# Scores of a two-head attention tile: the products of queries' high parts with keys' low parts move to 64 rows of TensorE each

## Chip, cores and metric

The kernel runs on one core of a Trainium2 chip. The metric is the device time of one launch in microseconds (us). The kernel before takes 1949.45 us, the median of three runs that lie between 1949.08 and 1949.52.

## What is computed

Two layers on 1024 tokens of width 1024, in float32: a gated short convolution and a SwiGLU feed-forward, then banded attention and a second feed-forward. The change lies in the attention. Each of 16 query heads has 64 channels; four query heads share one of four key heads; a block of 128 queries sees its own block of keys and the one before.

```python
    q = rmsnorm(q, q_gain)
    k = rmsnorm(k, k_gain)
    ...
    scores = jnp.einsum('bnqkgd,bnskd->bnkgqs', qb, kw).astype(jnp.float32) * scale
    ...
    logits = jnp.concatenate([scores, sink_col], axis=-1)
    p = jax.nn.softmax(logits, axis=-1)[..., :-1]
    out = jnp.einsum('bnkgqs,bnskd->bnqkgd', p.astype(vw.dtype), vw)
    out = out.reshape(bsz, s, N_Q_HEADS * HEAD_DIM)
    return out @ w_o
```

## The kernel before

**Split products.** TensorE multiplies in the type fp32r, which keeps less than float32. So each float32 matrix is split into a high part (rounded to fp32r) and a low part (the rest), and a product is the sum of high x high, high x low and low x high. `product_step` does this for one 128-row slice of the sum: six 128x512 matmuls, high weights on the two halves of the tokens with the operand's high part, again with its low part (L165), and the low weights with the high part (L169). `product` is a generator that hands back control after every two matmuls. The two halves of the tokens (512 columns each) go to two banks of PSUM that carry the tag `acc`; there are four of these, taken in turn, so that one product is summed while the other's two banks are read. Four other banks are called P0 to P3.

**A query tile.** The queries are projected in eight tiles i of 128 channels, each of which holds two heads e = 0 and 1 (64 channels each). `keep_q` copies the projected tile out of its two `acc` banks (`squares`, L1653, and `copy`, L1643, both on ScalarE), scales it by the heads' norms, and makes one operand for each head: 128 rows, of which the head's own 64 (rows 0 to 63 for e = 0, 64 to 127 for e = 1) hold the high part of its queries, and the other 64 the low part of the same queries. The keys stand twice, on rows 0 to 63 and on rows 64 to 127, as high part `hi` and low part `lo`.

**Scores.** `scores(i, b)` makes the scores of both heads of tile i for query block b, into the two halves of bank P0. For each head it issues two matmuls of 128 rows by 256 keys: the operand with `hi` (L1724), which gives high x high and low x high at once, and the operand with `lo` (L1725), which gives high x low and, as a by-product, low x low. There are 8 x 8 = 64 such units (i, b), so 256 matmuls. VectorE reads the scores in `maxima` (L1746, one instruction for each head, with the distance bias, the mask and the running minimum). Then ScalarE makes the exponents (L1764), TensorE transposes them (`turn`, L1776) into P1 or P3, ScalarE and VectorE split them (L1783, L1789), TensorE multiplies them with the values (L1801, L1802) into P2, and `keep_o` adds the two results (L1818, L1819).

**Order.** The attention's main part is ordered by hand: the program order of TensorE, VectorE, ScalarE and GpSimd is the order in which the code issues. `step` is called eight times for each query tile. It issues the scores of unit n, the transposes of unit n - 2 and the value products of unit n - 3 (LAG sets how the units run behind the projections), and between these three pieces of the running projection (P in the string below, two matmuls each). `plan(d, f)` puts f into an agenda d steps ahead; a whole number is issued at the end of that step (K), one with .5 in its middle (k).

```python
ORDER = "SPTZMEDkPHLBVOPK"
```

The letters are: S scores, T transposes, Z the preparation of the next score buffer, M maxima, E exponents, D divisions, H and L the split of the exponents, B the blanking of a column, V value products, O their sum.

For query tiles 1 to 7 the projection of tile i runs beside the attention of the tiles before. When it is done, the first half of the output projection follows: eight tiles m of output channels, each a product over the four operands in `o_split`, four steps for each m, with `add_x` (L282, VectorE) adding the two banks to the residual. `split_o` (L1912 on ScalarE, L1913 on GpSimd) makes those operands, in the room of the projections' operands XS0 to XS2 while query tile 7 is still being projected. Other tiles' head norms use `head_stats` (L1513, matmuls of two columns) and `turn_blocks` (L1601, transposes).

Of the kernel before, what the change touches and what calls it, by code (L numbers as in the profile page):

```python
# [10 lines left out]
F32 = mybir.dt.float32  # L11
# [70 lines left out]
def trunk_kernel(ctx: ExitStack, tc: tile.TileContext, xT, small, w_in, w_out, w_qk, w_v, w_o, w_gu, w_dn, out):  # L82
# [2 lines left out]
    pm = ctx.enter_context(tc.tile_pool(name="pm", bufs=1, space=bass.MemoryType.PSUM))  # L85
    dve, act, pool, pe = nc.vector, nc.scalar, nc.gpsimd, nc.tensor
    uid = [0]

    def slot(tag, shape=(P, D), dtype=F32, bufs=1):
        uid[0] += 1  # L90
# [4 lines left out]

    def bank(tag):
        uid[0] += 1
        return pm.tile([P, 512], F32, tag=tag, name=f"{tag}_{uid[0]}", bufs=4 if tag == "acc" else 1)

    def plain(ap):  # L100
        return ap.bitcast(F32)
# [40 lines left out]
    def load_w(src, n, hi_eng=act, lo_eng=dve):  # L142
        w = Weights()
        w.load(src, 0, n)
        w.split(0, n, hi_eng, lo_eng)
        return w
# [3 lines left out]
    class Acc:  # L150


        def __init__(self, tags=("acc", "acc")):
            self.parts = [(bank(tags[h]), slice(h * 512, h * 512 + 512)) for h in (0, 1)]

        def half(self, h):
            return self.parts[h][0]
# [1 line left out]
    def product_step(ps, w, xs, k, first, last):  # L159
        wh = w.hi[:, k * P : (k + 1) * P]  # L160
        wl = w.lo[:, k * P : (k + 1) * P]
        for j in (0, 1):
            for h in (0, 1):
                c = slice(h * 512, h * 512 + 512)
                pe.matmul(ps.half(h), wh, xs[:, j, c], start=first and j == 0, stop=False)  # L165
            yield
        for h in (0, 1):
            c = slice(h * 512, h * 512 + 512)
            pe.matmul(ps.half(h), wl, xs[:, 0, c], start=False, stop=last)  # L169
        yield  # L170

    def product(ps, w, operands, n=None):
        n = n or len(operands)
        for k in range(n):
            yield from product_step(ps, w, operands[k], k, k == 0, k == n - 1)

    def run(gen):
        for _ in gen:
# [1319 lines left out]
    def attention_layer():  # L1498
# [136 lines left out]
        def keep_q(i, acc):  # L1635

            t = {}

            def copy(h):
                if h == 0:  # L1640
                    t["raw"] = slot("G7") if i + 1 < NK else t["both"][:, 0, :]
                src, c = acc.parts[h]
                act.copy(t["raw"][:, c], src)  # L1643

            def squares(h):
                if h == 0:
                    if i + 1 < NK:
                        side = slot(f"G{5 + i % 2}")
                    else:
                        t["both"] = slot("XS5", (P, 2, D))  # L1650
                        side = t["both"][:, 1, :]
                    t["side"] = [side[:, h * 512 : h * 512 + 512] for h in (0, 1)]
                act.activation(t["side"][h], acc.half(h), AF.Square)  # L1653

            def stats_of():
                t["st"] = bank(pos["free"])
                for h in (0, 1):
                    head_stats(t["st"], t["side"][h], 4 * h, 4)

            def mean():  # L1660
                t["m"] = head_mean(t["st"])
                t["y"] = head_log(t["m"])

            def guess():
                t["t"] = head_guess(t["y"], cst[:, C_INVS + 2 * i : C_INVS + 2 * i + 2])

            def newton():
                head_newton(t["y"], t["t"], t["m"])


            def halves(e):
                rows = [slice(0, HD), slice(HD, P)]
                return rows[e], rows[1 - e]

            def part_hi(h, e):
                rows, _ = halves(e)
                if h == 0 and e == 0:
                    Q[i] = [slot(f"G{3 + i % 2}", dtype=F32R), slot(f"G{5 + i % 2}", dtype=F32R)]
                c = slice(h * 512, h * 512 + 512)
                dve.tensor_copy(Q[i][e][rows, c], t["raw"][rows, c])  # L1680

            def part_lo(h, e):
                rows, rest = halves(e)
                c = slice(h * 512, h * 512 + 512)
                q = Q[i][e]
                pool.tensor_tensor(q[rest, c], t["raw"][rows, c], plain(q)[rows, c], ALU.subtract)

            rows_of = lambda h: scale_rows(t["raw"], t["side"][h], h, bank(pos["free"]))
            wide_of = lambda h: spread(act, t["side"][h], t["y"][:, 4 * h : 4 * h + 4, :])

            first, rows = (1, (4.5, 5.5)) if i + 1 < NK else (0, (5.5, 6.5))
            for d, fs in (
                (first, [lambda: squares(0)]),
                (first + 0.5, [lambda: squares(1)]),
                (1.5 + first, [stats_of, mean]),
                (2 + first, [guess, newton]),
                (rows[0] - 1.5 if first else 0, [lambda: copy(0)]),
                (rows[0] - 1, [lambda: wide_of(0)]),
                (rows[0] - 0.5 if first else 1, [lambda: copy(1)]),
                (rows[0], [lambda: wide_of(1)]),  # L1700
                (rows[0], [lambda: rows_of(0)]),
                (rows[1], [lambda: rows_of(1)]),
                (rows[1], [lambda: part_hi(0, 0), lambda: part_hi(0, 1)]),
                (rows[1] + 0.5, [lambda: part_lo(0, 0)]),
                (rows[1] + 1, [lambda: part_lo(0, 1)]),
                (rows[1] + 1.5, [lambda: part_hi(1, 0), lambda: part_hi(1, 1), lambda: part_lo(1, 0)]),
                (rows[1] + 2.5, [lambda: part_lo(1, 1)]),
            ):
                for f in fs:
                    plan(d, f)  # L1710

        def key_blocks(b):
            return [1] if b == 0 else [0, 1]

        def scores(i, b):
            hi, lo = kz[i // 4]
            g = i % 2
            k0 = max(b - 1, 0)
            n = (b + 1 - k0) * P
            t = slice(b * P, (b + 1) * P)  # L1720
            kc = slice(k0 * P, (k0 + 2) * P)
            ps = bank("P0").rearrange("p (e c) -> p e c", e=2)
            for e, q in enumerate(Q[i]):
                pe.matmul(ps[:, e, :], q[:, t], hi[:, g, kc], start=True, stop=False)  # L1724
                pe.matmul(ps[:, e, :], q[:, t], lo[:, g, kc], start=False, stop=True)  # L1725
            S[i, b] = {"ps": ps, "n": n}


# [9 lines left out]
        def maxima(i, b):  # L1738
            u = S[i, b]
            s = u["s"] = s_bufs[(i * NB + b) % 3]  # L1740
            lo = 2 * P - u["n"]
            skip = 1 if lo == 0 else 0
            mx = u["mx"] = slot("mx", (P, 2), bufs=3)
            for e in range(2):
                h = 2 * i + e
                dve.tensor_tensor_reduce(  # L1746
                    s[:, e, lo + skip :],
                    u["ps"][:, e, skip : u["n"]],
                    dist[:, lo + skip :],
                    cst[:, C_NEGS + h : C_NEGS + h + 1],  # L1750
                    sinks[:, h : h + 1],
                    ALU.add,
                    ALU.min,
                    mx[:, e : e + 1],
                )
# [197 lines left out]
        E = mybir.EngineType  # L1953
        with tc.manual_schedule(engines={E.PE, E.Activation, E.DVE, E.Pool}):
            keep_q(0, acc)
            w = load_w(w_qk[1], NK, dve, pool)

            def load_next(i):
# [6 lines left out]

            w_after = load_next(2)
            for i in range(1, NK):
                acc = Acc()
                work = product(acc, w, xs)
                for k in range(NK):  # L1970
                    if k == 0:
                        w_next, w_after = w_after, None
                        n_next = NK if i + 1 < NK else len(early)
                    if k == 4 and i + 1 < NK:
                        w_after = load_next(i + 2)
                    if i == 6 and k == 2:
                        split_o(0, "A0", 0)
                    if i == 7 and k in (1, 3, 5):
                        split_o((k + 1) // 2, f"XS{k // 2}", 0)
                    step(work)  # L1980
                    if k in (0, 2, 3, 5):
                        j = 2 * (0, 2, 3, 5).index(k)
                        if j < n_next:
                            w_next.split(j, 2, act, pool)
                run(work)
                keep_q(i, acc)
                w = w_next
# [2 lines left out]
            free = ["XS3", "XS4"]  # L1990
            first_w = {}
            for m in range(NK):
                acc = Acc()
                work = product(acc, w, o_split, len(early))
                for k in range(len(early)):
                    if m + 1 < NK and k == 0:
                        w_next = Weights()
# [21 lines left out]
            while agenda:  # L2019
                planned_early()  # L2020
                planned()

        begin_with = []
        for e in (0, 1):
# [116 lines left out]
```

## Time and profile before

| | |
|---|---|
| median of three runs | 1949.45 us (1949.08 to 1949.52) |
| the profiled execution | 1950.02 us, span 1948.3 us |
| TensorE matmuls, busy share of the span | 99% |
| TensorE weight loads (beside the matmuls) | 83% |
| VectorE | 71% |
| ScalarE | 44% |
| GpSimd | 13% |
| attention's scores (L1724) | first at 1042.7 us, last at 1251.0 us |

PE is TensorE's matmul side and PEld its weight-load side; DVE is VectorE, ACT ScalarE, POOL GpSimd. A matmul's recorded time runs from its start to the end of its result, so neighbouring matmuls overlap in the record: what a stream of them costs is the distance from one start to the next. A time before a source line's group is busy time, then the mean of one instruction in ns, then the idle time ahead of it and what ended it.

### The profile page before, as it was taken

Reading aid. Unit: us, or ns where it says so; the run is one execution under the profiler, and the core shown is the slowest. Engines: PE = TensorE matmul, PEld = TensorE weight load, DVE = VectorE, ACT = ScalarE, POOL = GpSimd, SP = SyncE. Lnnn points to the kernel's source line nnn. Section 1 sums busy time; section 2 is a strip of 40 time slices with the busy share of each in tenths; the row PEclk is TensorE's granted clock in tenths of the full one; section 3 lists DMA queues with packets and bytes.
Section 4 is the critical chain, followed back from the end, with each engine's and each line's share of the span. In section 5 each row is a group of like instructions: output and inputs, shape, how many; then the busy total and the mean of one; then the engine's idle time right before and its main releaser. Section 6 shows DMA issues by size and latency. Waiting matters only on the chain.

```text
span 1948.3 us, 25757 instructions
## 1 busy us (share of the span) xinstructions
PE 1938.1 (99%) x9153; PEld 1617.3 (83%) x9153; DVE 1389.9 (71%) x2520; ACT 861.4 (44%) x1678; POOL 249.7 (13%) x384
## 2 busy tenths in 40 slices
PE   9999999999999999999999999999999999999999
PEld 7888888888888888888898888888888888888887
DVE  8998767876767676675645887788676767675543
ACT  5543434533333335444435777656333333344432
POOL 0000011011111110000004454410111111110000
PEclk9999999999999999999999999999999999999999
DMA  8532185244565458976300000051454555388563
GB/s 312 169 98 87 65 301 185 86 161 173 175 205 185 162 177 284 329 258 208 100 22 23 23 12 18 28 194 60 168 194 170 176 205 178 126 284 278 191 229 102
DMA packets 143169, 311.81 MB, mean 160 GB/s; under 512 B 13888, under 2 KB 53952, under 8 KB 143040
## 3 DMA queue, kind: packets, MB, share of 16 engines
q1 hardware_dynamic: 118992, 225.71, 35.0%
q0 software_dynamic: 23904, 84.42, 11.8%
q8 instruction: 72, 1.18, 0.3%
q14 instruction: 57, 0.47, 0.1%
q10 hardware_dynamic: 144, 0.03, 0.0%
HBM read 219.40 MB, written 90.70 MB: 159 GB/s over the span
## 4 chain that ended last, share of the span: by engine, by line
PE 93%; DVE 4%; issue 1%; ACT 1%; DMA 1%; SPq 0%; DVEq 0%; ACTq 0%
PE acc L907 15%; PE acc L904 15%; PE acc L905 15%; PE P L904 9%; PE P L907 9%; PE P L905 9%; PE acc L165 6%; PE acc L169 3%; PE acc L1034 2%; PE acc L1032 2%; PE acc L1033 2%; PE P L1776 1%; PE P L1724 1%; PE P L1513 1%; PE P L1601 1%
## 5 line engine op out<-in xcount | busy, mean ns | idle before, releaser
L904 PE MATMUL acc<-XS,G 128*128 128x512 f32 x894 | 348.2, 389 | 0.0
L907 PE MATMUL acc<-XS,G 128*128 128x512 f32 x894 | 347.8, 389 | 0.0
L905 PE MATMUL acc<-XS,G 128*128 128x512 f32 x894 | 347.8, 389 | 0.0
L905 PEld LDWEIGHTS acc<-XS,G 128*128 128x128 f32 x894 | 167.8, 188 | 34.8
L907 PEld LDWEIGHTS acc<-XS,G 128*128 128x128 f32 x894 | 167.8, 188 | 34.8
L904 PEld LDWEIGHTS acc<-XS,G 128*128 128x128 f32 x894 | 167.8, 188 | 34.8
L905 PE MATMUL P<-A,G 128*128 128x512 f32 x502 | 195.3, 389 | 0.0
L904 PE MATMUL P<-A,G 128*128 128x512 f32 x502 | 195.3, 389 | 0.0
L907 PE MATMUL P<-A,G 128*128 128x512 f32 x502 | 195.3, 389 | 0.0
L904 PE MATMUL acc<-A,G 128*128 128x512 f32 x410 | 159.5, 389 | 0.0
L905 PE MATMUL acc<-A,G 128*128 128x512 f32 x410 | 159.5, 389 | 0.0
L907 PE MATMUL acc<-A,G 128*128 128x512 f32 x410 | 159.5, 389 | 0.0
L844 DVE TENSOR_TENSOR G<-WL,G 128x512 fp32r<-128x512 f32 x168 | 115.0, 685 | 53.0 <-ACT G L843 53.0
L165 PE MATMUL acc<-XS,WH 128*128 128x512 f32 x480 | 146.8, 405 | 0.9 <-ACT WH L137 0.8
L843 ACT CAST G<-WR 128x512 fp32r<-128x512 f32 (+1 forms) x198 | 119.7, 605 | 62.9 <-PE acc L907 27.7
L844 DVE TENSOR_TENSOR G<-WR,G 128x512 fp32r<-128x512 f32 (+1 forms) x198 | 131.9, 666 | 10.9 <-ACT G L843 10.5
L843 ACT CAST G<-WH 128x512 fp32r<-128x512 f32 (+1 forms) x156 | 93.7, 601 | 82.9 <-PE acc L907 38.1
L1204 ACT ACTIVATE G<-G 128x512 f32<-128x512 f32 x88 | 55.8, 634 | 162.0 <-DVE G L1275 157.9
L843 ACT CAST G<-WL 128x512 fp32r<-128x512 f32 x168 | 103.5, 616 | 37.4 <-DVE WL L787 33.6
L904 PE MATMUL P<-XS,G 128*128 128x512 f32 x290 | 112.9, 389 | 0.1
L907 PE MATMUL P<-XS,G 128*128 128x512 f32 x290 | 112.8, 389 | 0.0
L905 PE MATMUL P<-XS,G 128*128 128x512 f32 x290 | 112.8, 389 | 0.0
(318 smaller groups left out, 3914.6 us busy)
## 6 DMA issues: line engine op xcount, KB each, us to landing
G<-h SPq DMA_DIRECT2D x70, 512.0 KB, 5.3
h<-X POOLq DMA_DIRECT2D x44, 512.0 KB, 5.2
X<-in_w_dn SPq DMA_DIRECT2D x80, 256.0 KB, 3.5
s<-X POOLq DMA_DIRECT2D x40, 512.0 KB, 4.7
WR<-in_w_gu SPq DMA_DIRECT2D x36, 512.0 KB, 6.1
WH<-in_w_gu SPq DMA_DIRECT2D x36, 512.0 KB, 6.4
h<-X POOLq DMA_DIRECT2D x66, 256.0 KB, 4.1
WR<-s SPq DMA_DIRECT2D x52, 256.0 KB, 3.4
```

The costliest lines, as they stand in the source:

```text
L165: pe.matmul(ps.half(h), wh, xs[:, j, c], start=first and j == 0, stop=False)
L169: pe.matmul(ps.half(h), wl, xs[:, 0, c], start=False, stop=last)
L843: lambda: act.copy(out_hi, raw),
L844: lambda: lo_eng.tensor_tensor(out_lo, raw, plain(out_hi), ALU.subtract),
L904: pe.matmul(ps, w[:, 0, c], x[:, 0, :], start=start and e == 0, stop=False, skip_group_check=True)
L905: pe.matmul(ps, w[:, 0, c], x[:, 1, :], start=False, stop=False, skip_group_check=True)
L907: pe.matmul(ps, w[:, 1, c], x[:, 0, :], start=False, stop=last, skip_group_check=True)
L1032: pe.matmul(ps, hi[:, kc], xs[:, 0, c], start=k == 0, stop=False, skip_group_check=True)
L1033: pe.matmul(ps, hi[:, kc], xs[:, 1, c], start=False, stop=False, skip_group_check=True)
L1034: pe.matmul(ps, lo[:, kc], xs[:, 0, c], start=False, stop=k == n_op - 1, skip_group_check=True)
L1204: state["silu"] = act.activation(x, x, AF.Silu)
L1513: pe.matmul(st[:, o : o + 2], sq[:, b * P : (b + 1) * P], half, start=True, stop=True)
```

## The change

In `scores` the two high matmuls of 128 rows come first, head 0 into bank P0 and head 1 into another bank. Then the two matmuls with `lo` follow, each on 64 rows only: head 0's high query rows (0 to 63) with the copy of the keys' low part on rows 0 to 63, at row position 0 of TensorE, and head 1's on rows 64 to 127, at row position 64. They add to what the high matmuls put into the two banks. The by-product low x low is left out. The count of matmuls stays: four for each unit.

The second bank is one of the four `acc` banks, taken out of the rotation for the length of the attention's main part and put back at its end; the rotation is written out as four tags. The projections then have three banks. So they go half by half of the tokens (`product_by_halves`): all slices of the first half into one bank, then all of the second half into the next, again with two matmuls between handings-back. The query tile 7 goes in four pieces (first half slices 0 to 3, second half slices 0 to 3, and so on). `copy(0)` of `keep_q` is planned for step 2 in place of 3 (step 1 for tile 6, step 0 for tile 7 as before), and the three `split_o` beside query tile 7 move from steps 1, 3 and 5 to 3, 4 and 5.

```diff
+    acc_tags = deque(f"acc{i}" for i in range(4))
...
     def bank(tag):
         uid[0] += 1
-        return pm.tile([P, 512], F32, tag=tag, name=f"{tag}_{uid[0]}", bufs=4 if tag == "acc" else 1)
+        if tag == "acc":
+            tag = acc_tags[0]
+            acc_tags.rotate(-1)
+        return pm.tile([P, 512], F32, tag=tag, name=f"{tag}_{uid[0]}", bufs=1)
...
+    def product_by_halves(ps, w, operands, n, chunk):
+        i = 0
+        for k0 in range(0, n, chunk):
+            for h in (0, 1):
+                c = slice(h * 512, h * 512 + 512)
+                if k0 == 0:
+                    ps.parts.append((bank("acc"), c))
+                for k in range(k0, k0 + chunk):
+                    kc = slice(k * P, (k + 1) * P)
+                    for j, (wp, xp) in enumerate(((w.hi, 0), (w.hi, 1), (w.lo, 0))):
+                        pe.matmul(
+                            ps.half(h),
+                            wp[:, kc],
+                            operands[k][:, xp, c],
+                            start=k == 0 and j == 0,
+                            stop=k == n - 1 and j == 2,
+                        )
+                        if i % 2:
+                            yield
+                        i += 1
...
-                (rows[0] - 1.5 if first else 0, [lambda: copy(0)]),
+                (0 if i + 1 == NK else 1 if i + 2 == NK else 2, [lambda: copy(0)]),
...
+        score_tags = ["P0"]
...
-            ps = bank("P0").rearrange("p (e c) -> p e c", e=2)
+            ps = [bank(tag)[:, 0 : 2 * P] for tag in score_tags]
             for e, q in enumerate(Q[i]):
-                pe.matmul(ps[:, e, :], q[:, t], hi[:, g, kc], start=True, stop=False)
-                pe.matmul(ps[:, e, :], q[:, t], lo[:, g, kc], start=False, stop=True)
+                pe.matmul(ps[e], q[:, t], hi[:, g, kc], start=True, stop=False)
+            for e, q in enumerate(Q[i]):
+                rows = slice(e * HD, (e + 1) * HD)
+                pe.matmul(ps[e], q[rows, t], lo[rows, g, kc], start=False, stop=True, tile_position=(e * HD, 0))
...
-                    u["ps"][:, e, skip : u["n"]],
+                    u["ps"][e][:, skip : u["n"]],
...
+            score_tags.append(acc_tags.popleft())
...
-                acc = Acc()
-                work = product(acc, w, xs)
+                acc = Acc(())
+                work = product_by_halves(acc, w, xs, NK, NK if i + 1 < NK else NK // 2)
...
-                    if i == 7 and k in (1, 3, 5):
-                        split_o((k + 1) // 2, f"XS{k // 2}", 0)
+                    if i == 7 and k in (3, 4, 5):
+                        split_o(k - 2, f"XS{k - 3}", 0)
...
-                acc = Acc()
-                work = product(acc, w, o_split, len(early))
+                acc = Acc(())
+                work = product_by_halves(acc, w, o_split, len(early), len(early))
...
+            acc_tags.insert(1, score_tags.pop())
```

More of the change, by code (lines that the diff above doesn't have):

```diff
@@ L153, in __init__ @@
         def __init__(self, tags=("acc", "acc")):
-            self.parts = [(bank(tags[h]), slice(h * 512, h * 512 + 512)) for h in (0, 1)]
+            self.parts = [(bank(tags[h]), slice(h * 512, h * 512 + 512)) for h in range(len(tags))]
         def half(self, h):
```

## The prediction

> **What bounds the kernel now.** The page comes first: its busy times, its row of TensorE's granted clock and the shares of the chain that ended last.
>
> ```profile
> span 1948.3 us, 25757 instructions
> PE 1938.1 (99%) x9153; PEld 1617.3 (83%) x9153; DVE 1389.9 (71%) x2520; ACT 861.4 (44%) x1678; POOL 249.7 (13%) x384
> PEclk9999999999999999999999999999999999999999
> PE 93%; DVE 4%; issue 1%; ACT 1%; DMA 1%; SPq 0%; DVEq 0%; ACTq 0%
> ```
>
> TensorE is the bound of the whole program, at its full clock, and 93% of the chain is its matmuls. The change lies in one stage, so the stage decides. Two stretches of the attention's main part, by the view of windows, and what TensorE waited for from 1042 to 1265 us, by the view of waits:
>
> ```profile
> core 0: us, PE busy (x) PEld busy (x) DVE busy (x) ACT busy (x) POOL busy (x), PEclk, DMA share, GB/s
> 1090.00:1120.00 30.00, 29.78 (x202) 26.28 (x201) 25.40 (x80) 22.95 (x70) 12.85 (x24) 1.00 0.07 19
> 1120.00:1150.00 30.00, 29.62 (x203) 26.15 (x202) 23.08 (x77) 22.54 (x70) 13.45 (x22) 1.00 0.03 10
> ```
>
> ```profile
> engine line waited for: us in total, times, longest us
> PE P L1724 <- DVE mx L1746: 1.7, 4, 0.6
> PE P L1776 <- DVE G L1768: 1.0, 3, 0.5
> PE P L1776 <- DVE s L1768: 0.3, 1, 0.3
> PE P L1776 <- ACT G L1764: 0.2, 1, 0.2
> ```
>
> TensorE is 99% busy in both stretches, and its recorded waits in 223 us come to 3.2 us. VectorE, the next engine, is at 25.40/30 = 85% and 23.08/30 = 77%. So what TensorE loses here the kernel loses, nearly one for one; what TensorE gains passes on as long as VectorE stays below its limit.
>
> **The scores now.** By source line, and then in the timeline of the two sides of TensorE:
>
> ```profile
> L1724 PE MATMUL P<-A,G x128: 274/278/356, 1042.7 to 1251.0; 128*128 128x256 f32 x128
> L1725 PE MATMUL P<-A,G x128: 274/282/283, 1042.8 to 1251.1; 128*128 128x256 f32 x128
> ```
>
> ```profile
> 1124.49 0.28 PE L1724 MATMUL P<-A,G 128*128 128x256 f32 x1
> 1124.61 0.28 PE L1725 MATMUL P<-A,G 128*128 128x256 f32 x1
> 1124.72 0.28 PE L1724 MATMUL P<-A,G 128*128 128x256 f32 x1
> 1124.85 0.28 PE L1725 MATMUL P<-A,G 128*128 128x256 f32 x1
> 1124.96 0.63 PE L165 MATMUL acc<-XS,WH 128*128 128x512 f32 x2
> ```
>
> Four matmuls of a unit take 1124.96 - 1124.49 = 0.47 us, so 0.117 us from start to start, while one lasts 0.278 us from start to end: each runs into the one before. 64 units lie between 1042.7 and 1251.0 us, one every 208.3/63 = 3.31 us.
>
> **Part 1: the pair side by side.** If the two 64-row matmuls of a unit stream at the same time, they take the place of one, and a unit loses 0.117 us: 64 x 0.117 = 7.5 us less on TensorE. No row of before has two matmuls side by side, so this gain is bounded by 0 and 7.5 us.
>
> **Part 2: going to 64 rows and back.** Each unit now changes TensorE from matmuls that use 128 rows to matmuls that use 64, and back: 128 changes. Before has no matmul on 64 rows, so the price must be bounded. From below: nothing. The nearest small price is a weight load that is not drawn ahead of the matmul it serves. It shows where the form of the work changes, from the two-column matmuls to the projection, in the timeline:
>
> ```profile
> 1122.80 0.36 PE L1513 MATMUL P<-cst,G 128*128 128x2 f32 x2
> 1123.02 0.71 PE L165 MATMUL acc<-XS,WH 128*128 128x512 f32 x2
> ```
>
> ```profile
> 1122.99 0.30 PEld L165 LDWEIGHTS acc<-XS,WH 128*128 128x128 f32 x2
> 1124.27 0.19 PEld L1724 LDWEIGHTS P<-A,G 128*128 128x128 f32 x1
> 1124.85 0.31 PEld L165 LDWEIGHTS acc<-XS,WH 128*128 128x128 f32 x2
> ```
>
> At 1124.85 the load stands 0.11 us ahead of its matmul (1124.96), and the two matmuls take 0.63 us. At 1122.99 it is 0.03 us ahead, and the same two take 0.71: 0.08 us are lost. At 0.08 for each change a unit would come to 2 x 0.08 - 0.117 = +0.043 us, and 64 units to +2.8 us.
>
> The next price is the whole tail of a matmul. If matmuls of the other form may not enter until the last has left, the distance between starts grows from 0.117 to the duration, 0.278: 0.161 us for each change. A unit then comes to 2 x 0.161 - 0.117 = +0.205 us, and 64 units to **+13.1 us**. From above: the new form's load begins only after that, too. Where TensorE starts again after a wait, the loads show what one takes:
>
> ```profile
> 1127.50 0.19 PEld L1724 LDWEIGHTS P<-A,G 128*128 128x128 f32 x1 [0.72 <-PE P L1802]
> 1127.53 0.35 PE L1724 MATMUL P<-A,G 128*128 128x256 f32 x1 [0.32 <-DVE mx L1746]
> 1127.61 0.19 PEld L1725 LDWEIGHTS P<-A,G 128*128 128x128 f32 x1
> 1127.73 0.28 PE L1725 MATMUL P<-A,G 128*128 128x256 f32 x1
> ```
>
> The second load starts 0.11 us behind the first, though nothing else held it. With 0.11 us more for each change a unit is at 2 x (0.161 + 0.11) - 0.117 = +0.425 us, and 64 units are at +27.2 us.
>
> I take the middle one. Adjacent matmuls overlap by 0.161 us, which needs both on the same 128 rows and the same way out; the two forms end differently (one sum over 128 rows against two sums over 64, in two banks), and a load of 0.11 us fits into that tail. The break-even is a price of 0.117/2 = 0.058 us for a change, below even the 0.08 of the mildest row. The Trainium skill, "TensorEngine Tiling (Array Packing)", section "Key Properties", has a rule that speaks against this change: "Changing tiling mode (not just tile) drains the TensorE". It gives no time; no run of before has two modes, so the trace neither bears it out nor denies it, and by it the middle price or the upper one would hold.
>
> **Part 3: banks and order around it.** The projections issue the same matmuls with the same loads in another order, so nothing changes in their count. They have three banks in place of four, which adds waits: the second half of tile i + 1 takes the bank of tile i's first half, behind the squares and the copy on ScalarE; in the output projection, behind the add on VectorE.
>
> ```profile
> L1653 ACT ACTIVATE G<-acc 128x512 f32<-128x512 f32 x10 | 5.9, 588 | 0.0
> L1643 ACT COPY G<-acc 128x512 f32<-128x512 f32 x12 | 6.9, 577 | 0.0
> L282 DVE TENSOR_TENSOR X<-acc,X 128x512 f32<-128x512 f32 x14 | 9.0, 687 | 0.2
> ```
>
> For tiles 2 to 6 the copy is issued at the end of the third step and wanted at the start of the fifth: one step of 3.31 us covers its 0.58. Behind a wait there TensorE would hold the transposes and value products of that step, and with them ScalarE's and VectorE's next work. Only query tile 7 has no step between: squares and copy, 0.588 + 0.577 = 1.2 us, follow the sum of the values in the step before, and the next scores (0.47 us) and value products cover half; 0 to 1.2 us, once. In the output projection the add ends 1.4 us into the second of four steps and its bank is wanted at the third. The three `split_o` now lie in adjacent steps, but end before the output projection starts, as they did. On the other side each head's scores have a bank of their own, so that head 0 need not wait for VectorE's reading of head 1: of the 1.7 us of such waits above, some may go. I put the whole part at 0, between -1.7 and +3 us. No DMA is moved, and no queue passed.
>
> **Sum.** Span 1948.3 + 13.1 = 1961.4 us; the profiled execution has 1950.02 - 1948.3 = 1.7 us around its span, so 1963.1 us. It is 0.57 us above the median 1949.45, so the median becomes **1962.5 us**, 0.7% slower. About 0.2%, 3.9 us, is what a measurement of this kernel can tell from no change.
>
> **The rivals.**
>
> *Side by side, and the change of form is free* (33%). The matmuls overlap as now, and the pair takes one's time: -7.5 us, of which VectorE at 77 to 85% lets most through; taken at 6.5, 1943.0 us. For it: TensorE already keeps a load running under the matmul before it, so work on separate rows may mix as freely; and the pair's two banks keep the outputs apart. Against it: it needs a change below 0.03 us, and the mildest visible loss is 0.08. The Trainium skill, "TensorE: Matmul & The Clock Gate", section "Part 3: Packing small matmuls", reports that matmuls on different row groups start within about 4 ns of each other; before shows none, and by that rule alone the 7.5 us would be gained.
>
> *The weight loads bind, so nothing runs side by side* (12%). A unit still has four loads. The chain of waits has a stretch of matmuls with two columns, where only the load is left:
>
> ```profile
> 1121.47 1.70 PE P L1513 x16
> ```
>
> 1.70/16 = 0.106 us for each load and matmul, close to the 0.117 of the 256-column ones. If a 64-row load takes as long and loads go one by one, the pair takes 2 x 0.106 = 0.21 us against 0.23: -1.4 us, and with a change of form at little cost 1948 to 1951 us. The change then does not do what it says. It decides where a change costs under 0.05 us.
>
> *Tail and load in line* (13%): the upper price, +27.2 us, 1976.7 us. For it: both rows above exist; against it: loads are drawn ahead almost everywhere.
>
> **How the numbers follow.** The forecast has 40%; its own range, from +3 to +22 us (a change between 0.08 and 0.23 us), is 1953 to 1972. The last 2% are waits of part 3 that exceed their cover, slower too. Faster by over 0.2% is the first rival, 0.33; within 0.2% the second, 0.12; slower the rest, 0.55. The range that should hold 8 in 10 reaches from the full gain (1949.45 - 7.5 = 1942) to just short of tail and load in line (1976): it leaves out half of that case and little else.
>
> **What would show it.** If the forecast is right, the group of 64-row matmuls starts about 0.28 us behind the high ones, its two starts lie within some 0.02 us, and the next projection starts about 0.28 us behind; the stage from first to last score grows by some 13 us, and all other stages keep their lengths. The first rival shows as 0.12, 0 and 0.12 us between starts; the second as four starts 0.11 us apart; the last as gaps near 0.39 us with loads standing behind the ends. The prediction is wrong if the scores' own spacing does not carry the difference: if TensorE waits for ScalarE or VectorE at an `acc` bank, or if a stage outside attention moves.

## The result: 1965.12 us, and the profile after

The changed kernel takes 1965.12 us (median of four runs, 1963.5 to 1966.77) against 1949.43 us of before beside it (1949.08 to 1949.52): a ratio of 1.0081, 95% interval 1.0069 to 1.0093. It is 15.7 us slower; 13.1 were forecast. The page of after, its busy times and the chain's shares:

```profile
span 1964.4 us, 25709 instructions
PE 1956.1 (100%) x9153; PEld 1621.2 (83%) x9153; DVE 1392.6 (71%) x2520; ACT 862.6 (44%) x1678; POOL 250.2 (13%) x384
PE 95%; DVE 3%; DMA 1%; ACT 1%; issue 1%; DVEq 0%; ACTq 0%
```

As many matmuls as before, and 18 us more of busy time on TensorE (1956.1 against 1938.1). The scores by source line in after, with the lowest, median and highest duration in ns and then the first and last start; L1753 is the high product, L1756 the low product on 64 rows:

```profile
L1753 PE MATMUL P<-A,G x64: 274/278/415, 1042.0 to 1266.7; 128*128 128x256 f32 x64
L1753 PE MATMUL acc<-A,G x64: 274/280/415, 1042.1 to 1266.8; 128*128 128x256 f32 x64
L1756 PE MATMUL P<-A,G x64: 379/380/579, 1042.3 to 1267.0; 64*128 64x256 f32 x64
L1756 PE MATMUL acc<-A,G x64: 379/381/577, 1042.3 to 1267.0; 64*128 64x256 f32 x64
```

From first to last score the stage now takes 1266.7 - 1042.0 = 224.7 us, where it took 208.3: that growth of 16.4 us accounts for all of the span's (1964.4 - 1948.3 = 16.1). One unit in the timeline of after, first the matmuls, then the loads:

```profile
1125.75 0.28 PE L1753 MATMUL P<-A,G 128*128 128x256 f32 x1
1125.87 0.28 PE L1753 MATMUL acc<-A,G 128*128 128x256 f32 x1
1126.08 0.38 PE L1756 MATMUL P<-A,G 64*128 64x256 f32 x1
1126.08 0.38 PE L1756 MATMUL acc<-A,G 64*128 64x256 f32 x1
1126.39 0.73 PE L192 MATMUL acc<-XS,WH 128*128 128x512 f32 x2
```

```profile
1126.08 0.18 PEld L1756 LDWEIGHTS P<-A,G 64*128 64x128 f32 x1
1126.08 0.18 PEld L1756 LDWEIGHTS acc<-A,G 64*128 64x128 f32 x1
1126.39 0.30 PEld L192 LDWEIGHTS acc<-XS,WH 128*128 128x128 f32 x2
```

The two 64-row matmuls start at the same time, so the pair does run side by side. But it starts 0.21 us behind the second high product, not 0.12; its loads begin with it and not ahead of it, and so it lasts 0.38 us and not 0.28. I read the difference, 0.10 us, as the part of the load that no matmul covers. The projection behind it stands as late again (0.31 us), with its load uncovered (0.73 us for two, where 0.63 was the rule). Leaving those 0.10 us out of the starts, a unit takes from 1125.75 to 1126.49, 0.74 us, where it took 0.47.

What TensorE still waits for in after, from 1042 to 1285 us:

```profile
PE P L1807 <- DVE G L1799: 1.1, 1, 1.1
PE acc L192 <- ACT G L1669: 0.4, 1, 0.4
```

The new waits for an `acc` bank come to 0.4 us in one place; the 3.2 us of waits of before have shrunk to 1.5.

### The profile page after: what moved, and what is told of

The parts are those of the page before. It is cut to its first block, busy times and chain, and to the rows that moved or that the text cites. A ratio compares the mean times of both kernels' runs of the same rounds, so it can differ in the third digit from the quotient of the medians.

```text
span 1964.4 us, 25709 instructions
## 1 busy us (share of the span) xinstructions
PE 1956.1 (100%) x9153; PEld 1621.2 (83%) x9153; DVE 1392.6 (71%) x2520; ACT 862.6 (44%) x1678; POOL 250.2 (13%) x384
## 4 chain that ended last, share of the span: by engine, by line
PE 95%; DVE 3%; DMA 1%; ACT 1%; issue 1%; DVEq 0%; ACTq 0%
PE acc L930 15%; PE acc L931 15%; PE acc L933 15%; PE P L930 9%; PE P L933 9%; PE P L931 9%; PE acc L192 6%; PE acc L169 2%; PE acc L1060 2%; PE acc L1058 2%; PE acc L1059 2%; PE P L1807 1%; PE acc L173 1%; PE P L1756 1%; PE P L1627 1%; PE P L1539 1%
## 5 line engine op out<-in xcount | busy, mean ns | idle before, releaser
L192 PE MATMUL acc<-XS,WH 128*128 128x512 f32 x320 | 117.7, 417 | 0.4 <-ACT G L1669 0.4
```

Source lines behind the costliest of these rows:

```text
L192: pe.matmul(ps.half(h), wp[:, kc], operands[k][:, xp, c], start=k == 0 and j == 0, stop=k == n - 1 and j == 2,)
```

## The experiments

Two theories can explain such a unit. *Change of form*: each going from 128 rows to 64 or back costs a tail and a load. *Own loads*: a 64-row matmul simply pays for its load each time. Beside them stands the question of whether the banks and the new order carry some of the loss, and what time on TensorE is worth at the end. All kernels start from the changed one; the edits lie in `scores`, but for the split of the norms' groups and the zero weights of the half-visit kernels, which are made outside it.

**Both low products on 128 rows again.**

```diff
-                rows = slice(e * HD, (e + 1) * HD)
-                pe.matmul(ps[e], q[rows, t], lo[rows, g, kc], start=False, stop=True, tile_position=(e * HD, 0))
+                pe.matmul(ps[e], q[:, t], lo[:, g, kc], start=False, stop=True)
```

> The change with its banks, halves and order, but the two low products on 128 rows each again, so that no matmul is on 64 rows. Theory 'change of form' (each visit to 64 rows costs two tails and two uncovered loads, the rest of the edit nothing): 1947 to 1950 us, no different from before or up to 2 us faster for the finer release of the score banks. Rival 'banks' (three banks and the order by halves carry the loss): 1958 us or more.

Measured: 1951.03 us against 1949.53 of before, ratio 1.0009, 1.0000 to 1.0017. So the banks and the order cost about 1.5 us, just outside the 1947 to 1950 expected, and the 64 rows the other 14.1. TensorE's waits in this kernel, 1030 to 1285 us, are where such a cost could show:

```profile
PE P L1806 <- DVE G L1798: 2.1, 4, 1.4
PE acc L192 <- ACT G L1669: 0.5, 1, 0.5
PE P L1806 <- DVE s L1798: 0.4, 1, 0.4
PE P L1753 <- DVE mx L1776: 0.3, 1, 0.3
PE acc L192 <- DVE X L308: 0.3, 1, 0.3
```

The waits for the score banks went from 1.7 to 0.3 us, as the finer release let one expect. 0.8 us for `acc` banks and 1.0 us more for the transposes (2.5 us at L1806 here, 1.5 at the same line of before, L1776) came in their place.

**No low products.**

```diff
             for e, q in enumerate(Q[i]):
-                pe.matmul(ps[e], q[:, t], hi[:, g, kc], start=True, stop=False)
-            for e, q in enumerate(Q[i]):
-                rows = slice(e * HD, (e + 1) * HD)
-                pe.matmul(ps[e], q[rows, t], lo[rows, g, kc], start=False, stop=True, tile_position=(e * HD, 0))
+                pe.matmul(ps[e], q[:, t], hi[:, g, kc], start=True, stop=True)
```

> As e1, with both low products left out altogether (the scores lack high x low). It tells what time saved on TensorE is worth here: 2 x 64 x 0.117 = 15 us of matmuls go. If it passes on one for one: 15 us below e1, about 1934 us. If VectorE takes its share: 1938 to 1945 us.

Measured: 1943.32 us, ratio to before 0.9968 (0.9956 to 0.9980). It is 7.7 us below the kernel with full rows, for 15 us of matmuls taken away: half passes on. Its view of waits, TensorE, same stretch:

```profile
PE P L1804 <- DVE G L1796: 3.8, 5, 1.6
PE P L1804 <- DVE s L1796: 1.5, 3, 0.9
PE P L1753 <- DVE mx L1774: 0.9, 2, 0.6
PE acc L192 <- ACT G L1669: 0.7, 1, 0.7
...
```

All its lines come to 8.6 us, 5.0 more than the 3.6 with full rows; VectorE is the releaser of most (the transposes L1804 wait for its blanking of a column). So this stage is bound by two engines almost at once, and at this rate a pair with free changes of form, 7.5 us less on TensorE, would by estimate have brought some 4 us; no run shows it.

**One on 64 rows, alone.**

```diff
-            for e, q in enumerate(Q[i]):
-                rows = slice(e * HD, (e + 1) * HD)
-                pe.matmul(ps[e], q[rows, t], lo[rows, g, kc], start=False, stop=True, tile_position=(e * HD, 0))
+            pe.matmul(ps[1], Q[i][1][:, t], lo[:, g, kc], start=False, stop=True)
+            pe.matmul(ps[0], Q[i][0][0:HD, t], lo[0:HD, g, kc], start=False, stop=True, tile_position=(0, 0))
```

> Head 1's low product on 128 rows, then head 0's alone on 64: one visit for each unit as in the change, but no pair. Theory 'change of form': the visit costs what it did and the second matmul is no longer beside it, so 64 x 0.117 = 7.5 us more than the change, 1971 to 1973 us. Rival 'own loads' (each 64-row matmul pays for its own load and nothing is paid for the change of form): half of the price goes, 1956 to 1959 us.

Measured: 1972.36 us (1970.55 to 1974.79), ratio 1.0118 (1.0104 to 1.0131), 7.2 us more than the change. Its timeline:

```profile
1162.72 0.28 PE L1753 MATMUL acc<-A,G 128*128 128x256 f32 x1
1162.84 0.28 PE L1754 MATMUL acc<-A,G 128*128 128x256 f32 x1
1163.05 0.38 PE L1755 MATMUL P<-A,G 64*128 64x256 f32 x1
1163.36 0.73 PE L192 MATMUL acc<-XS,WH 128*128 128x512 f32 x2
```

One 64-row matmul has the same 0.21, 0.31 and 0.38 as a pair. The price hangs on the visit and not on each matmul's load, and the pair's second matmul was free: the 7.2 us agree with head 1's low product standing in line on 128 rows (64 x 0.117 = 7.5).

**The pair twice in one visit.**

```diff
-            for e, q in enumerate(Q[i]):
-                rows = slice(e * HD, (e + 1) * HD)
-                pe.matmul(ps[e], q[rows, t], lo[rows, g, kc], start=False, stop=True, tile_position=(e * HD, 0))
+            for last in (False, True):
+                for e, q in enumerate(Q[i]):
+                    rows = slice(e * HD, (e + 1) * HD)
+                    pe.matmul(ps[e], q[rows, t], lo[rows, g, kc], start=False, stop=last, tile_position=(e * HD, 0))
```

> The pair on 64 rows is issued twice within one visit (the low product counts twice in the scores). Theory 'change of form': a second pair costs its streaming alone, 0.117 us if its two matmuls run side by side and their loads are drawn ahead: 64 x 0.117 = 7.5 us more than the change, 1971 to 1973 us. If the matmuls of a pair run one behind the other: 15 us more, 1978 to 1981. Rival 'own loads': the second pair costs as much as the first, 64 x 0.3 = 19 us or more, from 1983 us.

Measured: 1970.56 us (1970.03 to 1971.37), ratio 1.0107 (1.0092 to 1.0123), 5.4 us more than the change, a little under the 7.5 expected and far from 15 or 19. Matmuls, then loads:

```profile
1161.65 0.38 PE L1757 MATMUL P<-A,G 64*128 64x256 f32 x1
1161.66 0.38 PE L1757 MATMUL acc<-A,G 64*128 64x256 f32 x1
1161.88 0.28 PE L1757 MATMUL P<-A,G 64*128 64x256 f32 x1
1161.88 0.28 PE L1757 MATMUL acc<-A,G 64*128 64x256 f32 x1
1162.09 0.73 PE L192 MATMUL acc<-XS,WH 128*128 128x512 f32 x2
```

```profile
1161.76 0.19 PEld L1757 LDWEIGHTS P<-A,G 64*128 64x128 f32 x1
1161.77 0.19 PEld L1757 LDWEIGHTS acc<-A,G 64*128 64x128 f32 x1
```

Within the visit the second pair's loads stand 0.11 to 0.12 us ahead of it, both at once, and it lasts the usual 0.28. So loads on separate rows run side by side too, and only the matmuls that follow a change pay.

**High and low in turn: four changes for each unit.**

```diff
             for e, q in enumerate(Q[i]):
+                rows = slice(e * HD, (e + 1) * HD)
                 pe.matmul(ps[e], q[:, t], hi[:, g, kc], start=True, stop=False)
-            for e, q in enumerate(Q[i]):
-                rows = slice(e * HD, (e + 1) * HD)
                 pe.matmul(ps[e], q[rows, t], lo[rows, g, kc], start=False, stop=True, tile_position=(e * HD, 0))
```

> High and low product in turn for each head: 128 rows, 64, 128, 64. Four changes of form for each unit in place of two, and nothing side by side. Theory 'change of form': two more changes of 0.19 us and 0.117 us for the lost pair, 0.50 us for a unit, 64 x 0.50 = 32 us more than the change, 1990 to 1998 us, and more dips of the granted clock. Theory 'own loads': the same loads as in the change, 1965 to 1973 us.

Measured: 1995.41 us (1992.75 to 2005.08), ratio 1.0230 (1.0212 to 1.0247), 30.3 us more than the change.

```profile
1161.02 0.28 PE L1754 MATMUL P<-A,G 128*128 128x256 f32 x1
1161.22 0.38 PE L1755 MATMUL P<-A,G 64*128 64x256 f32 x1
1161.53 0.38 PE L1754 MATMUL acc<-A,G 128*128 128x256 f32 x1
1161.85 0.38 PE L1755 MATMUL acc<-A,G 64*128 64x256 f32 x1
1162.16 0.73 PE L192 MATMUL acc<-XS,WH 128*128 128x512 f32 x2
```

As above, the listed start of a matmul of 0.38 us is taken as that of its uncovered load, and its own as 0.10 us later. So from start to start the five stand 0.30, 0.31, 0.32 and 0.31 us apart, in both directions, where 0.117 is the rule: some 0.195 us for each change.

**Half the visits, and its control.** Two query blocks' scores are made at once, in the two whole banks of 512 columns (`both`). A matmul with zero weights (`none[0]`) opens each bank, so that the two blocks can share it. In the control the last two lines are one matmul on 128 rows. The main lines in place of the two loops, for even b:

```diff
...
+            for e in range(2):
+                pe.matmul(both[e], none[0][:, 0:1].to_broadcast([P, P]), Q[i][0][:, 0:512], start=True, stop=False)
+            for u in (b, b + 1):
+                t, kc, c, n = parts(u)
+                for e, q in enumerate(Q[i]):
+                    pe.matmul(both[e][:, c], q[:, t], hi[:, g, kc], start=False, stop=False)
+                S[i, u] = {"ps": [both[e][:, c] for e in range(2)], "n": n}
+            for u in (b, b + 1):
+                t, kc, c, n = parts(u)
+                for e, q in enumerate(Q[i]):
+                    rows = slice(e * HD, (e + 1) * HD)
+                    pe.matmul(both[e][:, c], q[rows, t], lo[rows, g, kc], start=False, stop=u > b, tile_position=(e * HD, 0))
```

> The scores of two query blocks are made at once, every second step: four high products, then two pairs on 64 rows in one visit, so 32 visits in place of 64. So that two blocks can share a bank, a product with zero weights over all 512 columns opens each of the two banks (2 x 0.23 us for a visit, 15 us in all, the same in e7). To be set against e7. Theory 'change of form': 32 visits x 0.39 - 64 x 0.117 = 5 us more than e7, up to 7. Theory 'own loads': the same difference as between the change and e1, 14 us.

> As e6 with the low products on 128 rows: the control of e6. No visit to 64 rows; 64 opening products of 0.23 us, 15 us, stand on TensorE beyond e1. By what e2 showed (half of what TensorE saves is kept) between 7 and 15 us more than e1: 1958 to 1966 us.

Measured: 1968.84 us (ratio 1.0098, 1.0083 to 1.0113) against 1964.22 us of the control (1.0075, 1.0060 to 1.0090). Halving the visits brings the price of the 64 rows from 14.1 us down to 4.6; 5 were expected. The control is 13.2 us above the kernel with full rows for 64 x 0.23 = 15 us of added matmuls: what is added to TensorE here passes on almost whole, what is taken away only by half. (The control also makes its scores every second step; what that alone costs was not run.)

**Two groups of norms in place of one.** The profiled execution of the change has two dips of TensorE's granted clock, which the prediction knew nothing of. The windows of after that hold them (the clock stands behind the five engines: 0.75, 0.91, 0.94, 0.72), matmuls inside the second, and the two groups of two-column matmuls (head norms, `head_stats`) nearest to them:

```profile
1045.00:1050.00 5.00, 5.00 (x27) 4.12 (x27) 2.41 (x10) 3.37 (x12) 2.08 (x7) 0.75 0.00 0
1050.00:1055.00 5.00, 5.00 (x28) 3.99 (x28) 2.95 (x12) 3.08 (x9) 0.19 (x1) 0.91 0.00 0
...
1125.00:1130.00 5.00, 5.00 (x35) 4.38 (x35) 2.47 (x9) 2.67 (x9) 0.87 (x2) 0.94 0.00 0
1130.00:1135.00 5.00, 5.00 (x24) 4.04 (x23) 3.58 (x12) 3.31 (x12) 0.90 (x2) 0.72 0.00 0
```

```profile
1045.31 1.84 PE L1539 MATMUL P<-cst,G 128*128 128x2 f32 x16
...
1127.39 1.84 PE L1539 MATMUL P<-cst,G 128*128 128x2 f32 x16
...
1129.84 0.41 PE L1832 MATMUL P<-G,A 128*128 128x256 f32 x1
1130.06 0.41 PE L1833 MATMUL P<-G,A 128*128 128x256 f32 x1
```

Each dip loses 5 x (0.25 + 0.09) = 5 x (0.06 + 0.28) = 1.7 us, and each begins at or right behind a group of 16 two-column matmuls. The edit, in the change and in the kernel with high and low in turn; `stats_of(h)` now issues 8 of the 16:

```diff
...
-                (1.5 + first, [stats_of, mean]),
-                (2 + first, [guess, newton]),
+                (1.5 + first, [lambda: stats_of(0)]),
+                (2 + first, [lambda: stats_of(1), mean, guess, newton]),
```

> The change, with the 16 two-column matmuls of each query tile's head norms issued in two groups of 8, half a step apart, with projection and value products between. In the profile of the change both dips of the granted clock begin during or right behind such a group of 16 (1.84 us from 1045.31 and 1127.39 us). Theory 'low work in a window' (a visit's gaps and the group together let the clock drop): the dips go or become rare, mean clock 0.999 to 1.000 in nearly all executions, 1962 to 1964.5 us. Rival 'changes of form alone': executions at 0.998 remain, median 1964 to 1966 us.

> The same split of the groups of 16 with high and low products in turn (four changes of form for each unit), where the clock fell most. Theory 'low work in a window': fewer dips than without the split, mean clock mostly 0.999 to 1.000, 1990 to 1993 us. Rival 'changes of form alone': clocks between 0.993 and 1.000 as before, 1992 to 2005 us.

> The changed kernel once more, beside the two kernels with split groups on the same chip: 1963 to 1967 us, mean clock 0.998 to 1.000. It gives the spread to set the split against.

Measured: split 1964.37 us (1963.99 to 1965.04), ratio 1.0078 (1.0065 to 1.0090), mean clock 1.000 in all five executions; the change beside it 1965.32 us (1964.34 to 1965.73), ratio 1.0082 (1.0068 to 1.0095), clock 0.998 or 0.999 in all four. In turn with the split: 1994.46 us (1993.48 to 1995.42), ratio 1.0233 (1.0218 to 1.0249), 1.5 us above the range expected, clock 0.999 or 1.000 where it had been as low as 0.993. The clock answers to the split as the first theory has it; the times don't tell the theories apart: 1964.37 lies in both ranges expected, and the median gains 1 us at most, within the spread of both.

## Why the prediction was right, and where its sizes were off

*TensorE bounds the stage*: right in the main for added work (13.2 of 15 us in the control, 14.1 of the 17.3 of Part 2 below). For saved work it was too kind. The first rival let "most" of 7.5 us through; the kernel without low products shows half.

*Part 1, the pair side by side*: right, at its upper bound. Both matmuls start 3 to 4 ns apart in all 64 units of after, and taking one out of the pair costs 7.2 us where 7.5 were to be lost. By that the second rival falls: loads of a pair begin together, as the twice-issued pair shows. The Trainium skill, "TensorE: Matmul & The Clock Gate", section "Part 3: Packing small matmuls", with its some 4 ns between starts, agrees with this.

*Part 2, the change of form*: this is what decided, and the term that was mis-sized. 0.161 us were taken for each change; 0.195 were measured, the same into 64 rows and out of them. The mechanism lies between the middle price and the upper one: the new form's load does not fit into the tail (the step that failed), but it does not wait for the tail's end either. The sign named for the forecast, 0.28 us between starts with the load covered, did not come; it is 0.31. The load begins some 0.07 us ahead of the recorded end (1126.08 against 1125.87 + 0.28 = 1126.15), and 0.10 us of it are uncovered. Matmul ends are modelled in the record, so the division between tail and load is not shown, only their sum. A unit thus costs 0.27 us more on TensorE, not 0.205: 17.3 us in place of 13.1. The Trainium skill, "TensorEngine Tiling (Array Packing)", section "Key Properties", has a change of tiling mode drain TensorE; 0.195 us at each change, in both directions, agrees with that rule. The last rival's 0.27 us a change is too much.

*Part 3, banks and order*: put at 0, between -1.7 and +3; measured 1.5, with an interval that reaches from 0 to 3.3. The finer release gained its 1.4 us in waits, as allowed for, and the `acc` banks cost 0.4 to 0.8.

*The sum* was 15.7 against 13.1 us. In the profiled execution Part 2 adds 17.3 us, banks and order 1.5 and the two dips 3.4: 22.2, of which 16.1 arrive in its span. Some 6 us are taken up where TensorE waits in the kernel with full rows. The view of waits shows 2.1 of these (3.6 us there, 1.5 in after). It leaves out a matmul that starts late but still within the recorded tail of the one before. Counting by how much later than usual for their shapes TensorE's matmuls start, from 1040 to 1290 us and outside the dips, I find 9.0 us in the trace with full rows and 4.1 in after: by this estimate some 5 of the 6. That the median came within 2.6 us of the forecast (1965.12 against 1962.5) is therefore in part luck: the change of form was put 4.2 us too low and the dips and Part 3 at nothing, but not all of it arrived.

## What to carry to other kernels

A change of TensorE's row tiling has a price for each visit, not for each matmul: here two times 0.195 us. A visit must save more than that. By this estimate at least four pairs of 256 columns (0.117 us saved by each) belong in one visit before packing pays; one pair cost 14.1 us here, two pairs a visit still 4.6, and four were not run. Before taking time off the bounding engine, leave the work out once: that shows in one run how much of the saving another engine would take back.

## What was not expected of the hardware

TensorE's granted clock fell though its matmul side was recorded as busy without a gap (5.00 of 5.00 us in each of the four windows above). Inside a dip 256 columns take 0.22 us in place of 0.117, near half speed. Mean clocks of single executions: before always 1.000; full rows 1.000 but for one of eleven at 0.999, and the control with opening products but for one of four; 32 visits 1.000; 64 visits 0.997 to 1.000; 128 visits (in turn) 0.993 to 1.000. So in these runs the dips grow with the changes of form, and much of the changed kernel's spread goes with them: it took 1963.5 us at a clock of 1.000, and 1966.14 and 1966.77 at 0.998. With the norms' groups split they are gone from the changed kernel (1.000 in all five executions) and fewer with high and low in turn (0.999 or 1.000, where 0.993 had been the lowest). The Trainium skill, "TensorE: Matmul & The Clock Gate", section "Part 1: The HAM clock gate (the "warmup" mystery)", describes a gate between full and half clock that follows how busy the array was in windows of some 3.4 us; half speed and 1.7 us lost agree with one such window each. That tails, uncovered loads and two-column matmuls count there as little work fits these runs, but it is not shown: the count itself is in no record.

The other surprise is that loads on separate rows of TensorE run side by side like the matmuls: both loads of a pair begin within 0.01 us, and in the twice-issued pair the second pair stands only 0.12 us behind the first.
